# Sample rows of the ending ordered as (token, quarter) instead of (quarter, token)

## The chip, the cores and the metric

The kernel runs on one core of one Trainium2 chip. The metric is device time in microseconds, the median of repeated executions. Beside it there is one profiled execution of the kernel before, whose trace gives the time of every instruction and DMA packet.

## The reference

One step of a decoder layer on 256 prompt tokens and 32 sample tokens (8 sequences of 4 tokens), with 2048 features each. The two groups differ only in the state that they start from; the layer's last line is what the change touches:

```python
merged = jax.nn.sigmoid(m_a) * y_a + jax.nn.sigmoid(m_b) * y_b
x = layer_norm(ALPHA * x + merged @ w_o, ln1_g, ln1_b)
hid = jnp.square(jax.nn.relu(x @ w_up))
x = layer_norm(ALPHA * x + hid @ w_down, ln2_g, ln2_b)
...
def layer_norm(x, g, b):
    mu = jnp.mean(xf, -1, keepdims=True)
    var = jnp.mean(jnp.square(xf - mu), -1, keepdims=True)
    return ((xf - mu) * lax.rsqrt(var + LN_EPS) * g + b)
```

The results of this line are `y_prompt` (256 rows of 2048 floats, 2 MB) and `y_sample` (8 x 4 rows of 2048 floats, 256 KB). The convolution states and the delta-rule states are results too, and are stored much earlier.

## The kernel before

The kernel is one long stream of weight blocks. `add_group` lists them in order; each block is a 512 KB transfer on SP's queue (L171), a split of its floats into a high part on ScalarE (L179) and a low part on VectorE (L140), and three TensorE products for each 128 x 128 piece (L206 to L208). Activations lie with the features on the 128 partitions and the 288 tokens (256 of the prompt, then 32 samples) along the free axis. The order of the work is written out by hand: `at` and `due` say after which block a piece of other work is recorded, and each engine runs what it was given in that order.

The last layer norm needs the tokens on the partitions, so the features' tiles are turned by TensorE as they become ready. For the prompt this gives two tiles of 128 tokens x 2048 features. The 32 sample tokens would fill only 32 partitions; the kernel therefore packs them as 128 rows of 512 features, one row for each pair of a token and a quarter of the features. This packing is what the change reorders. Its steps, all in the ending:

- `tail_consts` (L561 on) loads, on GpSimd's queue, the scale and the shift of the layer norm. It is recorded 60 blocks before the last quarter of the `w_down` stream; GpSimd has nothing else to do by then and runs ahead of it. For the sample rows, `gs` and `bs` hold for each of the 128 rows the 512 values of its quarter.
- `sample_copy(w)` (L621, L622) copies 4 x 32 sample columns of `acc` to 128 columns of `cs` on ScalarE, four times; only `sample_copy(3)` has to wait for the last block.
- `sample_turn` turns these 128 x 128 pieces on TensorE (L627), takes their statistics (L631) and multiplies them by `gs`.
- `final` (from L648) combines the four rows of a token by a 128 x 128 matrix of quarters, `quart` (L722, L733), and ends with the sample rows' scaling (L740 on ScalarE, L741 on GpSimd, and VectorE's last instruction, recorded under its helper's line L143) and with their store, issued from ScalarE's queue (L750). The prompt's rows are stored from SP's queue: two stores of 512 KB (L708) and four of 256 KB (L713).

At the end of the program SP waits for the completion of each of these stores, one after the other (L1452).

Of the kernel before, what the change touches and what calls it, by code (L numbers as in the profile page):

```python
# [16 lines left out]
P = 128  # L17
D = 2048
NP_ = 256
NS = 32  # L20
NT = NP_ + NS
# [19 lines left out]
def _constants():  # L41
    k = np.arange(P)[:, None]
    m = np.arange(P)[None, :]
    f = {}
    f["ident"] = k == m
    f["lcum"] = (k <= m) & (k // 64 == m // 64)
    f["lrem"] = (k > m) & (k // 64 == m // 64)
    f["ones"] = np.ones((P, P))
    f["hm"] = k // 64 == m // 64
    i = np.arange(64)[None, :]  # L50
    f["lc"] = (k % 64) <= i
    f["mbias"] = np.where((k % 64) <= i, 0.0, -1e30)
    f["mask8"] = (k % 64) // 8 == i // 8
    f["i8"] = k % 8 == np.arange(8)[None, :]
    f["i8u"] = k % 8 < np.arange(8)[None, :]
    f["bo8"] = k // 8 == m // 8
    ks = k - 96
    mt = m % 32
    inb = (ks >= 0) & (ks // 4 == mt // 4)
    f["lcums"] = inb & (ks <= mt)  # L60
    f["lrems"] = inb & (ks > mt)
    f["lsp"] = ks == mt
    same = k // 4 == m // 4
    f["l4"] = same & (k <= m)
    f["mbias4"] = np.where(same & (k <= m), 0.0, -1e30)
    f["mask1s"] = same & (k % 2 == 0) & (m == k + 1)
    f["sel"] = (k // 32) == (np.arange(8)[None, :] % 4)
    f["bm3"] = (ks >= 0) & (ks // 4 == np.arange(8)[None, :])
    f["bmask"] = (k % 32) // 4 == np.arange(8)[None, :]
    f["hmask"] = (k // 64) == np.arange(2)[None, :]  # L70
    f["nlow"] = -np.concatenate([k // 64 == 1, (k // 32) % 2 == 1], 1).astype(np.float32)
    offs, cols, o = {}, [], 0
    f["quart"] = (k % 32 == m % 32) * 0.25
    f["rowhi"] = np.isin(k, (0, 2, 3, 5)) * 1.0
    f["rowlo"] = np.isin(k, (1, 4)) * 1.0
    early = ("hm", "bo8", "lcum", "lrem", "lcums", "lrems", "lsp", "bm3", "hmask")
    late = ("quart", "rowhi", "rowlo")
    for n, a in [(n, a) for n, a in f.items() if n not in early + late] + [(n, f[n]) for n in early + late]:
        if n in (early[0], late[0]):
            offs["early" if n == early[0] else "late"] = o  # L80
        a = np.broadcast_to(np.asarray(a, np.float32), (P, a.shape[1]))
        offs[n] = (o, o + a.shape[1])
        o += a.shape[1]
        cols.append(a)
    fm = np.ascontiguousarray(np.concatenate(cols, 1), dtype=np.float32)
    g = {}
    j = k % 64
    for s in (8, 16, 32):
        g[s] = (j // (2 * s) == i // (2 * s)) & ((j // s) % 2 == 0) & ((i // s) % 2 == 1)
    g["s"] = same & ((k // 2) % 2 == 0) & ((m // 2) % 2 == 1)  # L90
    io, cols, o = {}, [], 0
    for n, a in g.items():
        io[n] = (o, o + a.shape[1])
        o += a.shape[1]
        cols.append(np.asarray(a, np.int32))
    im = np.ascontiguousarray(np.concatenate(cols, 1), dtype=np.int32)
    return fm, offs, im, io


CF, CF_AT, CI, CI_AT = _constants()  # L100


@with_exitstack
def hybrid_kernel(ctx: ExitStack, tc: tile.TileContext, A):
# [31 lines left out]
    act, dve, pe, gps, sp = nc.scalar, nc.vector, nc.tensor, nc.gpsimd, nc.sync  # L136
# [5 lines left out]
    def stt(out, a, s, b, o0, o1):  # L142
        dve.scalar_tensor_tensor(out=out, in0=a, scalar=s, in1=b, op0=o0, op1=o1)  # L143
# [77 lines left out]
    ph = {}  # L221
# [325 lines left out]
    def collect(ps):  # L547
        turned(14)
        fin, bn = ph["fin"], ph["bn"]
        for b in range(2):  # L550
            dve.bn_aggr(out=fin[:, b, 1:3], in_=bn[:, b, 0:15])
        dve.tensor_scalar(out=fin[:, :, 2], in0=fin[:, :, 2], scalar1=15.0 * P, scalar2=None, op0=MUL)

        R = ph["R"] = ph["pool"].tile([P, 2, 2, 6], F32R, tag="mv", name="R")
        act.copy(R[:, 1, :, 3:5], bc(ones[:, 0:2], 2))
        act.mul(R[:, 1, :, 5], ones[:, 0:2], 0.0)
        sample_copy(2)
        idle = lambda: None
        fill.extend([idle] * 5 + [lambda: sample_turn(2, 3)])

    def tail_consts():  # L561
        g3 = ph["pool"].tile([P, KT, NT], F32, tag="R2", name="g3").rearrange("p k t -> p (k t)")
        ph["g2"] = g3[:, 0:D]
        ph["gs"], ph["bs"], ph["b0"] = (g3[:, D + 512 * u:D + 512 * u + 512] for u in range(3))
        ph["late"] = g3[:, D + 1536:D + 1536 + CF.shape[1] - NL]
        gps.dma_start(ph["g2"][:, 1024:D], A["ln2_g"][:, 1024:D].to_broadcast([P, D - 1024]))
        gps.dma_start(ph["b0"], A["ln2_b"][:, 1024:1536].to_broadcast([P, 512]))
        gps.dma_start(ph["late"], A["cf"][:, NL:])
        for j in range(4):
            for t, n in (("gs", "ln2_g"), ("bs", "ln2_b")):  # L570
                gps.dma_start(ph[t][32 * j:32 * j + 32, :], A[n][:, 512 * j:512 * j + 512].to_broadcast([32, 512]))

    def tail_tiles():
        pl = ph["pool"]
# [44 lines left out]


    def sample_copy(w):  # L621
        act.copy(ph["cs"][:, w * P:w * P + P].rearrange("p (j t) -> p j t", j=4), ph["acc"][:, w::4, NP_:NT])  # L622

    def sample_turn(w0, w1, split=False):
        g = gtile()[:, 0:(w1 - w0) * P]
# [15 lines left out]
    def out_tiles(p):  # L641
        for u in range(2):
            turned(2 * p + u)
        if p == 6:
            sample_copy(0)
            sample_copy(1)

    def final(ps):  # L648
        a, fin, sm, Y, Ys, R = ph["acc"], ph["fin"], ph["sm"], ph["Y"], ph["Ys"], ph["R"]
# [26 lines left out]
        m = mv[:, :, 0]  # L676
# [70 lines left out]
        dve_unit(0, 3, r03)  # L747
        dve_unit(1, 3, r13)
        stt(Ys, ph["gs"], ts, Ys, MUL, ADD)
        act.dma_start(A["y_sample"].rearrange("b t (j f) -> j (b t) f", j=4), Ys)  # L750

    mark["up"] = len(blocks)
    for c in range(4):
# [586 lines left out]
    t = raw.pop(0)  # L1340
# [31 lines left out]
    for i in range(3, len(blocks)):  # L1372
# [47 lines left out]
        if i == mark["down3"] - 60:  # L1420
            tail_consts()
# [34 lines left out]
```

## Time and profile before

| | |
|---|---|
| median of 3 executions | 1706.29 us (1705.9 to 1706.83) |
| the profiled execution: time | 1707.11 us |
| the profiled execution: span of the trace | 1705.3 us |
| TensorE busy | 1688.1 us, 99% of the span |
| VectorE, ScalarE, GpSimd busy | 59%, 43%, 8% |

The span is the time from the first to the last instruction in the trace; what the execution's time has beyond it, 1.8 us, lies outside the trace. Times inside the trace count from the span's start. A queue's row gives its packets, the megabytes that they carried, and the share of the 16 DMA engines' time that they took; q1 carries SP's transfers, q10 those of ScalarE, q0 those of GpSimd.

### The profile page before, as it was taken

Reading aid. Unit: us, or ns where it says so; the run is one execution under the profiler, and the core shown is the slowest. Engines: PE = TensorE matmul, PEld = TensorE weight load, DVE = VectorE, ACT = ScalarE, POOL = GpSimd, SP = SyncE. Lnnn points to the kernel's source line nnn. Section 1 sums busy time; section 2 is a strip of 40 time slices with the busy share of each in tenths; the row PEclk is TensorE's granted clock in tenths of the full one; section 3 lists DMA queues with packets and bytes.
Section 4 is the critical chain, followed back from the end, with each engine's and each line's share of the span. In section 5 each row is a group of like instructions: output and inputs, shape, how many; then the busy total and the mean of one; then the engine's idle time right before and its main releaser. Section 6 shows DMA issues by size and latency. Waiting matters only on the chain.

```text
span 1705.3 us, 31096 instructions
## 1 busy us (share of the span) xinstructions
PE 1688.1 (99%) x13063; PEld 1669.0 (98%) x13063; DVE 1008.3 (59%) x1297; ACT 734.5 (43%) x1068; POOL 131.3 (8%) x220
## 2 busy tenths in 40 slices
PE   9999999999999999999999999999999999999996
PEld 7999999999999999999999999999999999999996
DVE  4577885757544445556788744565445654466564
ACT  4775536334543333344445533344334433344432
POOL 2232421023300000000010000000000000000000
PEclk8999999999999999999999999999999999999998
DMA  8464366435655555555565555555555555555551
GB/s 243 139 196 138 123 190 201 148 112 168 182 164 171 161 167 167 162 161 163 171 185 171 169 163 167 167 161 167 168 161 164 169 161 169 165 161 165 166 158 63
DMA packets 274654, 279.18 MB, mean 164 GB/s; under 512 B 13072, under 2 KB 269521, under 8 KB 274509
## 3 DMA queue, kind: packets, MB, share of 16 engines
q1 hardware_dynamic: 270126, 265.82, 50.3%
q0 software_dynamic: 4256, 11.12, 2.4%
q8 instruction: 102, 1.67, 0.4%
q10 hardware_dynamic: 132, 0.26, 0.1%
q14 instruction: 38, 0.30, 0.0%
HBM read 269.68 MB, written 7.48 MB: 163 GB/s over the span
## 4 chain that ended last, share of the span: by engine, by line
PE 98%; DMA 0%; DVE 0%; SPq 0%; issue 0%; ACT 0%
PE acc L206 31%; PE acc L208 31%; PE acc L207 31%; PE g L1085 1%; DMA xr<-in_x_prompt_dram 0%; PE g L1073 0%; PE g L1232 0%; PE g L1252 0%; PE g L1255 0%; PE g L832 0%; PE g L799 0%; PE g L606 0%; PE g L1204 0%; PE g L1244 0%; PE g L959 0%; PE g L800 0%
## 5 line engine op out<-in xcount | busy, mean ns | idle before, releaser
L140 DVE TENSOR_TENSOR lo<-raw,hi 128x1024 fp32r<-128x1024 f32 (+2 forms) x502 | 614.7, 1227 | 551.7 <-ACT hi L179 549.1
L179 ACT CAST hi<-raw 128x1024 fp32r<-128x1024 f32 (+1 forms) x498 | 517.5, 1041 | 761.7 <-PE acc L207 709.2
L206 PE MATMUL acc<-xh,hi 128*128 128x288 f32 x1408 | 422.6, 300 | 0.0
L208 PE MATMUL acc<-xh,lo 128*128 128x288 f32 x1408 | 416.8, 296 | 0.0
L207 PE MATMUL acc<-xl,hi 128*128 128x288 f32 x1408 | 416.5, 296 | 0.0
L206 PE MATMUL acc<-dh,hi 128*128 128x290 f32 x1024 | 303.9, 297 | 0.0
L207 PE MATMUL acc<-dl,hi 128*128 128x290 f32 x1024 | 303.3, 296 | 0.0
L208 PE MATMUL acc<-dh,lo 128*128 128x290 f32 x1024 | 302.7, 296 | 0.0
L208 PE MATMUL acc<-hh,lo 128*128 128x288 f32 x1024 | 302.3, 295 | 0.0
L206 PE MATMUL acc<-hh,hi 128*128 128x288 f32 x1024 | 302.3, 295 | 0.0
L207 PE MATMUL acc<-hl,hi 128*128 128x288 f32 x1024 | 302.2, 295 | 0.0
L206 PEld LDWEIGHTS acc<-xh,hi 128*128 128x128 f32 x1408 | 265.5, 189 | 2.4 <-issue 0.7
L207 PEld LDWEIGHTS acc<-xl,hi 128*128 128x128 f32 x1408 | 265.9, 189 | 0.9
L208 PEld LDWEIGHTS acc<-xh,lo 128*128 128x128 f32 x1408 | 265.6, 189 | 0.0
L206 PEld LDWEIGHTS acc<-dh,hi 128*128 128x128 f32 x1024 | 193.6, 189 | 0.1
L208 PEld LDWEIGHTS acc<-dh,lo 128*128 128x128 f32 x1024 | 193.3, 189 | 0.0
L207 PEld LDWEIGHTS acc<-dl,hi 128*128 128x128 f32 x1024 | 193.3, 189 | 0.1
L207 PEld LDWEIGHTS acc<-hl,hi 128*128 128x128 f32 x1024 | 192.4, 188 | 0.0
L208 PEld LDWEIGHTS acc<-hh,lo 128*128 128x128 f32 x1024 | 192.3, 188 | 0.0
L206 PEld LDWEIGHTS acc<-hh,hi 128*128 128x128 f32 x1024 | 192.1, 188 | 0.0
L207 PE MATMUL acc<-ml,hi 128*128 128x288 f32 x256 | 75.6, 295 | 0.0
L208 PE MATMUL acc<-mh,lo 128*128 128x288 f32 x256 | 75.6, 295 | 0.0
(402 smaller groups left out, 1619.8 us busy)
## 6 DMA issues: line engine op xcount, KB each, us to landing
raw<-in_w_in_dram SPq DMA_DIRECT2D x176, 512.0 KB, 3.5
raw<-in_w_up_dram SPq DMA_DIRECT2D x128, 512.0 KB, 3.8
raw<-in_w_down_dram SPq DMA_DIRECT2D x128, 512.0 KB, 3.6
raw<-in_w_o_dram SPq DMA_DIRECT2D x32, 512.0 KB, 3.6
raw<-in_w_a_out_dram SPq DMA_DIRECT2D x16, 512.0 KB, 3.7
raw<-in_w_b_out_dram SPq DMA_DIRECT2D x16, 512.0 KB, 3.6
S<-in_state_gdn_dram POOLq DMA_DIRECT2D x8, 512.0 KB, 7.5
out_dram<-S POOLq DMA_DIRECT2D x8, 512.0 KB, 4.4
```

The source lines that it names most:

```text
L140: dve.tensor_tensor(out=out, in0=a, in1=b, op=op)
L179: act.copy(his[i][:, k:k + step], raw[i][:, k:k + step])
L206: pe.matmul(o, wh, xh_, start=st, stop=False)
L207: pe.matmul(o, wh, xl_, start=False, stop=False)
L208: pe.matmul(o, wl, xh_, start=False, stop=en)
L1085: pe.matmul(out[r, q * 64:q * 64 + 64], a[r, q, :], b[r, q, :], start=True, stop=True)
```

## The change

The 128 sample rows are numbered as 4 x token + quarter instead of 32 x quarter + token. Four things follow from it: the matrix `quart` sums over neighbours instead of over rows 32 apart; the scale and the shift are loaded by one transfer each, whose source repeats the four quarters 32 times, instead of four transfers each; ScalarE's copy writes its 128 columns with a step of four floats instead of one after another; and the output is addressed as 128 rows of 512 floats that follow one another in memory, instead of as 4 x 32 rows with 8 KB between rows of one quarter.

```diff
-    f["quart"] = (k % 32 == m % 32) * 0.25
+    f["quart"] = (k // 4 == m // 4) * 0.25
...
-        for j in range(4):
-            for t, n in (("gs", "ln2_g"), ("bs", "ln2_b")):
-                gps.dma_start(ph[t][32 * j:32 * j + 32, :], A[n][:, 512 * j:512 * j + 512].to_broadcast([32, 512]))
+        for t, n in (("gs", "ln2_g"), ("bs", "ln2_b")):
+            gps.dma_start(ph[t], A[n].rearrange("o (j f) -> o j f", j=4).to_broadcast([NS, 4, 512]))
...
-        act.copy(ph["cs"][:, w * P:w * P + P].rearrange("p (j t) -> p j t", j=4), ph["acc"][:, w::4, NP_:NT])
+        act.copy(ph["cs"][:, w * P:w * P + P].rearrange("p (t j) -> p j t", j=4), ph["acc"][:, w::4, NP_:NT])
...
-        act.dma_start(A["y_sample"].rearrange("b t (j f) -> j (b t) f", j=4), Ys)
+        act.dma_start(A["y_sample"].rearrange("b t (j f) -> (b t j) f", j=4), Ys)
```

As built, the store's destination is [128 rows, 512 floats] where it was [4, 32, 512]; every engine has its instructions in the same order as before, but for GpSimd, which issues six loads fewer. The changed kernel has one source line less from L569 on, so that the store stands at L749.

## The prediction

> **What bounds the kernel now.** I read the page's chain first, then the end of the chain in order of time, then the stages of the ending, and last the DMA packets and the issues of the stores.
>
> ```profile
> span 1705.3 us, 31096 instructions
> q10 hardware_dynamic: 132, 0.26, 0.1%
> PE 98%; DMA 0%; DVE 0%; SPq 0%; issue 0%; ACT 0%
> ...
> 1692.88 0.74 DVE Y L143
> 1693.62 0.68 DVE r L143
> ```
>
> TensorE carries 98% of the chain and the change takes nothing from it. But the chain in order of time ends with VectorE at 1693.62 + 0.68 = 1694.30, 11 us before the span does. No engine computes in those 11 us. The stages of the ending show what they hold:
>
> ```profile
> core 0: us, PE busy (x) PEld busy (x) DVE busy (x) ACT busy (x) POOL busy (x), PEclk, DMA share, GB/s
> 1693.40:1697.60 4.20, 0.00 (x0) 0.00 (x0) 0.89 (x2) 0.00 (x0) 0.11 (x1) 0.50 0.96 362
> 1697.70:1698.90 1.20, 0.00 (x0) 0.00 (x0) 0.00 (x0) 0.00 (x0) 0.00 (x0) 0.50 0.37 41
> 1698.90:1700.90 2.00, 0.00 (x0) 0.00 (x0) 0.00 (x0) 0.00 (x0) 0.00 (x0) 0.50 0.69 167
> 1700.90:1702.60 1.70, 0.00 (x0) 0.00 (x0) 0.00 (x0) 0.00 (x0) 0.00 (x0) 0.50 0.22 83
> 1702.60:1703.84 1.24, 0.00 (x0) 0.00 (x0) 0.00 (x0) 0.00 (x0) 0.00 (x0) 0.50 0.09 36
> 1703.84:1705.30 1.46, 0.00 (x0) 0.00 (x0) 0.00 (x0) 0.00 (x0) 0.00 (x0) 0.50 0.00 0
> ```
>
> The last two columns are the busy share of the 16 DMA engines and the rate. Until 1697.6 they are full (0.96, 362 GB/s). Then comes a hole of 1.2 us at 41 GB/s, then two microseconds at 167, and from 1700.9 to 1703.84 a thin tail: 0.22 of 16 engines is 3.5 engines, 0.09 is 1.4. After the last packet 1.46 us of waits and drains follow. So the end is set by a few DMA engines that work on after the others are done. Which, the packets say. First the window of one prompt store alone (128 rows of 2 KB, issued from SP at 1690.54), then the thin tail:
>
> ```profile
> DMA packets 144, 0.26 MB, mean 97 GB/s; under 512 B 16, under 2 KB 16, under 8 KB 144
> q1 hardware_dynamic: 144, 0.26, 26.1%
> ...
> DMA packets 102, 0.19 MB, mean 42 GB/s; under 512 B 11, under 2 KB 11, under 8 KB 102
> q1 hardware_dynamic: 66, 0.12, 7.0%
> q10 hardware_dynamic: 36, 0.07, 4.0%
> ```
>
> The prompt store is 144 packets: 128 rows and 16 small ones. The sample store, of the same 128 rows and 0.26 MB, is 132 (the q10 row of the page): 128 rows and 4 small ones. I read a small packet as one engine's completion: the prompt store runs on 16 engines with 8 rows each, the sample store on 4 with 32 rows each. In the thin tail 11 small packets are left. Four engines that owe three stores each (the sample rows and the last two prompt stores) would owe 12; that fits, and so do the 3.5 engines above. The four do sample rows while the prompt rows in their queues wait, and the last prompt store ends at 1703.84 because of them.
>
> The Trainium skill ("DMA: Bandwidth & Descriptors", section "Why a DMA increments its semaphore by 16 and not by 1") gives the rule behind this: a transfer issued from SP or ScalarE uses the largest number of engines up to 16 that divides the slowest dimension of both sides, and each engine used posts one completion. By that rule [4, 32, 512] against 128 partitions takes 4 engines and [128, 512] takes 16; the 4 and 16 small packets above agree for the two shapes that this trace has.
>
> **The change part by part.**
>
> *The output's transfer.* It keeps its 128 rows, its place (ScalarE issues it behind VectorE's last instruction at 1694.3) and its queue. Its built form is that of the prompt store, 128 rows of 512 floats on both sides, so I take 16 engines with 8 rows each. Removed from each of the four engines: 32 - 8 = 24 rows. Added to each of the twelve: 8. One row costs 0.261 x 16 x 2.7 us = 11.3 us of engine time over 128 rows = 0.088 us (the prompt store's window, 2.7 us long). So the four lose 2.1 us and the twelve gain 0.70 us. What is late next is the twelve engines' own end, 1700.9 by the windows. How far that moves depends on the hole, and so on when the last prompt store's packets arrive:
>
> ```profile
> 1690.54 0.37 SPq L713 DMA_DIRECT2D out_dram<-Y  x1
> 1693.77 0.65 SPq L713 DMA_DIRECT2D out_dram<-Y  x1
> 1694.33 1.15 ACTq L750 DMA_DIRECT2D out_dram<-r  x1
> 1694.52 1.14 SPq L713 DMA_DIRECT2D out_dram<-Y  x1
> 1695.75 1.58 SPq L713 DMA_DIRECT2D out_dram<-Y  x1
> ```
>
> The same instruction takes 0.37 us on an idle queue, 0.65 us behind two 512 KB stores, and 1.14 and 1.58 us once the sample store is in the queue. No row shows it behind a 16-engine sample store. The bounds are 0.65 us (the delay came from four engines that could not take 32 rows each) and 1.58 us (it comes from two queues issuing at once). I take 0.65, as it is the nearest row: a store of this form behind a full backlog of 16-engine stores. Then the last issue ends at 1695.75 + 0.65 = 1696.40 instead of 1697.33, 0.93 us earlier, and its packets could begin at 1698.9 - 0.93 = 1697.97. Before them each engine now has 8 sample rows: the full stretch ends at 1697.6 + 0.70 = 1698.30, so the last store begins there, 0.60 earlier than now, with no hole. Its eight rows per engine take 0.70 us at the pace of the lone store, or the 2.0 us that the twelve took (1698.9 to 1700.9). Ends: 1699.0 or 1700.3; bytes give a check: 41 x 1.2 + 167 x 2.0 + 83 x 1.7 + 36 x 1.24 = 569 KB are left at 1697.7, and at 362 GB/s that is 1.57 us, end 1699.3. I take the middle, 1699.7. Gain: 1703.84 - 1699.7 = 4.1 us, between 3.5 and 4.8. The 1.46 us behind the last packet stay, since the same stores are waited for.
>
> *The loads of scale and shift.*
>
> ```profile
> L571 POOL DMA_DIRECT2D g<-in_ln_g_dram x4: 496/497/518, 864.1 to 870.9; - x4
> L571 POOL DMA_DIRECT2D g<-in_ln_b_dram x4: 496/498/515, 864.6 to 871.4; - x4
> POOL r L588 <- PE acc L207: 707.7, 1, 707.7
> ```
>
> Eight issues of 0.5 us become two, so 3 us of GpSimd's time go, for the same 512 KB. GpSimd then waits 707.7 us for TensorE (the third row, who waited for whom): nothing is queued behind them, and the values are needed 800 us later. Worth 0; without that cover it would be the 3 us. The stream of weights passes there with the same bytes: 0.
>
> *ScalarE's copy with a step of four floats.*
>
> ```profile
> L179 ACT CAST hi<-raw 128x1024 fp32r<-128x1024 f32 x492 | 514.1, 1046 | 757.5 <-PE acc L207 709.2 <-issue 39.2 <-ACT hi L179 8.7
> L179 ACT CAST hi<-raw 128x512 fp32r<-128x512 f32 x6 | 3.4, 619 | 4.2 <-DMA raw<-in_w_in_dram 4.2
> L622 ACT COPY r<-acc x4: 293/298/300, 1674.3 to 1685.8; 128x128 f32<-128x128 f32 x4
> ...
> PEld g L686 <- DVE R L140: 0.4, 1, 0.4
> ```
>
> An element costs (1046 - 619) / 512 = 0.83 ns, so 128 of them 0.107 us of the copy's 0.298. No row here has this step. Bounds: no change, or each element twice, +0.11 us for each of four copies; it cannot gain, as the count stays. Only the last copy, at 1685.8, has TensorE behind it, and there TensorE waits 0.4 us for VectorE's R soon after (the last row), which takes up 0.11. I take 0; without that cover +0.1.
> The Trainium skill speaks against this part ("SBUF — State Buffer", section "Door 1: The DMA port swizzle"): full rate needs at least two consecutive accesses to one 16-byte line, and each step to a new line pays. A step of four floats is a new line every time; the page has no price for it, so by it the sum would lose the 0.1 us that the doubled copy stands for, if the cover failed. No run here shows the penalty.
>
> *The matrix of quarters, the turns, statistics and scalings* keep their shapes and their order: 0.
>
> Sum: -4.1 us. The profiled execution would go from 1707.11 to 1703.0, with a span of 1701.2. Its time stands 0.82 above the median 1706.29, so the median comes to 1702.2.
>
> **The rivals.**
>
> *The issues stay slow.* The hole is due to two queues issuing at once, whatever the shape; for it speaks that the 1.14 us issue overlaps ScalarE's own of 1.15 us almost wholly, against it that the 1.58 us one comes when ScalarE's is over. Then the last store's packets come at 1698.9 as now, and the twelve engines' end stays: 1700.9 if the 8 added rows fit in the hole (0.70 in 1.2 us), 1701.6 if they follow. Gain 2.9 to 2.2 us, median 1703.4 to 1704.1.
>
> *The path to memory is slow, not the engines.* After the hole the rate is 167 GB/s even while more than four engines work (share 0.69). If that is the limit, spreading the rows does not raise it: 569 - 49 = 520 KB after 1698.9 take 3.1 us, end 1702.0, gain 1.8 us, median 1704.5. Against it: 362 GB/s before the hole, of the same kind of stores.
>
> *Slower: the store falls on one engine.* Its destination is now one run of 256 KB. If it went out as such, from one engine, 128 x 0.088 = 11.3 us and two prompt stores' 16 rows (1.4 us) from 1697.0 on end at 1709.7: 5.9 us later, median 1712.2. It decides only at one engine; on two, 64 + 16 rows end at 1704.0, no change. Against it: the built form has 128 rows on both sides, as the 144-packet store has.
>
> *The change doesn't do what it says* (still four engines): gain 0; against it, the same built form.
>
> **How the numbers follow.** Some 0.2%, 3.4 us, is what a measurement of this kernel can tell from no change. Chances: forecast 0.58 (3.5 to 4.8 us, all over the bound), issues stay slow 0.26, slow path 0.09, no change 0.03, one engine 0.04. So faster 0.58, same 0.38, slower 0.04. The forecast's own range is 1701.5 to 1702.8; the range goes to 1701.0 for the executions' spread (0.4 to 0.5 us to either side) and at the other end over the slow issues to 1704.4, which leaves out the last three.
>
> **What would show it.** Right: q10 with 144 packets, 16 of them small; no tail below four engines' share; the last L713 issue near 0.65 us and no hole after 1697.6; last packet near 1699.7; ScalarE's copy at 0.30 us. Wrong: 132 packets, or fewer; the last issue still at 1.6 us with the hole in place, which would be the second case; a hole gone but a rate near 167 GB/s, the third.

## The result

The changed kernel takes 1702.06 us (median of 11 executions, 1700.99 to 1702.92), the kernel before 1705.9 us beside it (11 executions): a ratio of 0.9977, 95% interval 0.9968 to 0.9986, so 3.8 us less. The profiled execution took 1702.91 us, with a span of 1701.1 us. The page's first line, and its row for ScalarE's queue:

```profile
span 1701.1 us, 31087 instructions
...
q10 hardware_dynamic: 144, 0.26, 0.0%
```

The sample store is now 128 rows and 16 small packets, where it had 4. The stages of the ending, cut at the times used before (last two columns: share of the 16 DMA engines, GB/s):

```profile
core 0: us, PE busy (x) PEld busy (x) DVE busy (x) ACT busy (x) POOL busy (x), PEclk, DMA share, GB/s
1693.40:1697.60 4.20, 0.00 (x0) 0.00 (x0) 1.21 (x2) 0.22 (x1) 0.42 (x1) 0.50 0.89 345
1697.70:1698.90 1.20, 0.00 (x0) 0.00 (x0) 0.00 (x0) 0.00 (x0) 0.00 (x0) 0.50 1.03 382
1698.90:1700.90 2.00, 0.00 (x0) 0.00 (x0) 0.00 (x0) 0.00 (x0) 0.00 (x0) 0.50 0.20 76
1700.90:1702.60 1.70, 0.00 (x0) 0.00 (x0) 0.00 (x0) 0.00 (x0) 0.00 (x0) 0.50 0.00 0
```

The second row was the hole: it went from 41 to 382 GB/s. The tail after 1700.9 is empty. Cut where this kernel's own work begins and ends:

```profile
1692.60:1693.70 1.10, 0.31 (x1) 0.00 (x0) 1.10 (x2) 1.02 (x2) 1.10 (x1) 0.50 0.00 0
...
1697.60:1699.44 1.84, 0.00 (x0) 0.00 (x0) 0.00 (x0) 0.00 (x0) 0.00 (x0) 0.50 0.95 352
1699.44:1701.10 1.66, 0.00 (x0) 0.00 (x0) 0.00 (x0) 0.00 (x0) 0.00 (x0) 0.50 0.00 0
```

The engines are full to the last packet at 1699.44, which was at 1703.84. The waits and drains behind it take 1.66 us, 0.2 more than before. Of the issues of the stores, only ScalarE's fell back to the idle queue's 0.37 us; the last one from SP, at 1696.06, takes 1.12 us:

```profile
1694.08 0.66 SPq L712 DMA_DIRECT2D out_dram<-Y  x1
1694.64 0.37 ACTq L749 DMA_DIRECT2D out_dram<-r  x1
1694.84 1.14 SPq L712 DMA_DIRECT2D out_dram<-Y  x1
1696.06 1.12 SPq L712 DMA_DIRECT2D out_dram<-Y  x1
```

One part of the change costs something. First the copy's row, TensorE's turn behind it and GpSimd's loads; then the chain's last line:

```profile
L621 ACT COPY r<-acc x4: 414/422/428, 1674.5 to 1686.1; 128x128 f32<-128x128 f32 x4
...
1686.52 0.33 PE L626 MATMUL g<-cf,r 128*128 128x128 f32 x1 [0.21 <-ACT r L621]
...
1689.68 0.15 DVE L140 TENSOR_TENSOR r<-r,g 128x1 f32<-128x1 f32 x1
...
L570 POOL DMA_DIRECT2D g<-in_ln_g_dram x1: 566/566/566, 864.3 to 864.3; - x1
L570 POOL DMA_DIRECT2D g<-in_ln_b_dram x1: 588/588/588, 864.9 to 864.9; - x1
...
1693.92 0.68 DVE r L143
```

Each copy takes 0.42 us where it took 0.30, and TensorE waits 0.21 us for the last one. VectorE ends at 1694.60, 0.30 us later than before. Of this, 0.20 is there already at VectorE's first instruction behind the last block and comes from the long stream, as other traces differ too. The other 0.10 enters at VectorE's small instruction of 1689.68 (before: 1689.38): it reads the product of `quart`, which TensorE runs in order behind the late turn.

### The profile page after: what moved, and what is told of

Its sections match the earlier page's. It is cut to its first block, busy times and chain, and to the rows that moved or that the text cites. A ratio compares the mean times of both kernels' runs of the same rounds, so it can differ in the third digit from the quotient of the medians.

```text
span 1701.1 us, 31087 instructions
## 1 busy us (share of the span) xinstructions
PE 1688.0 (99%) x13063; PEld 1669.1 (98%) x13063; DVE 1008.2 (59%) x1297; ACT 734.5 (43%) x1068; POOL 128.3 (8%) x214
## 4 chain that ended last, share of the span: by engine, by line
PE 98%; DMA 0%; DVE 0%; SPq 0%; issue 0%; ACT 0%
PE acc L206 31%; PE acc L208 31%; PE acc L207 31%; PE g L1084 1%; DMA xr<-in_x_prompt_dram 0%; PE g L1072 0%; PE g L1231 0%; PE g L1251 0%; PE g L1254 0%; PE g L831 0%; PE g L798 0%; PE g L605 0%; PE g L1203 0%; PE g L1243 0%; PE g L958 0%; PE g L799 0%
```

## The experiments

The long stream, which no edit here touches, ends up to 2.8 us apart from trace to trace (the first 512 KB prompt store is issued between 1690.90 and 1693.68), so the endings are compared by the time from the issue of the first 512 KB prompt store to the last packet. It is 11.1 us in the kernel before (1692.76 to 1703.84) and 6.4 us in the changed one (1693.07 to 1699.44).

**The old rows on 16 engines.** The kernel before with one edit:

```diff
-        act.dma_start(A["y_sample"].rearrange("b t (j f) -> j (b t) f", j=4), Ys)
+        ys = A["y_sample"].rearrange("b t (j f) -> j (b t) f", j=4)
+        for j in range(4):
+            act.dma_start(ys[j], Ys[32 * j:32 * j + 32, :])
```

> The kernel before, with its old row order, its eight loads and its copy, but the sample store cut into four stores of 32 rows each (one quarter each, still 8 KB between rows), so that each has 32 rows on both sides and, by my theory, runs on 16 engines with 2 rows each. Theory (the number of engines is the whole gain): no tail after the hole, last packet near 1699.4, median 1702.0, some 3.8 us under the kernel before; q10 shows 128 rows and 64 small packets. Rival (the gain comes from rows that follow one another in memory): the rows are 8 KB apart as before, so the tail stays and the median is that of the kernel before, 1705.9, or above it for three more issues of 0.37 us.

Measured: 1702.5 us against 1706.3 us, ratio 0.9976 (0.9967 to 0.9986), the changed kernel's gain. Its q10 row and its stages:

```profile
q10 hardware_dynamic: 192, 0.26, 0.1%
...
1693.40:1697.60 4.20, 0.00 (x0) 0.00 (x0) 0.80 (x2) 0.00 (x0) 0.01 (x1) 0.50 0.99 354
1697.60:1699.64 2.04, 0.00 (x0) 0.00 (x0) 0.00 (x0) 0.00 (x0) 0.00 (x0) 0.50 0.89 300
1699.64:1701.20 1.56, 0.00 (x0) 0.00 (x0) 0.00 (x0) 0.00 (x0) 0.00 (x0) 0.50 0.00 0
```

192 packets are 128 rows and 4 x 16 small ones. The ending is 7.0 us, with rows still 8 KB apart and no hole. So 4.1 of the 4.7 us by which the changed kernel's ending is shorter come without rows that follow one another in memory, and without the row order, the loads and the copy of the change. The ending stays 0.6 us longer than the changed kernel's, at 300 GB/s to the end where that has 352; whether this is the rows' distance or the four issues from ScalarE, no run parts.

**The new rows on 4 engines.** The changed kernel with

```diff
-        act.dma_start(A["y_sample"].rearrange("b t (j f) -> (b t j) f", j=4), Ys)
+        ys = A["y_sample"].rearrange("b t (j f) -> (b t j) f", j=4)
+        for r in (slice(0, 124), slice(124, P)):
+            act.dma_start(ys[r], Ys[r, :])
```

> The changed kernel with its new row order, loads and copy, but the store cut into rows 0 to 123 and rows 124 to 127. Neither 124 nor 4 is divided by a number from 5 to 16, so each should run on 4 engines: 31 rows and 1 row on each, in memory one after another. Theory (number of engines): the tail of four engines is back, last packet near 1703.9, median 1706.0 (that of the kernel before, and 0.1 us for the slower copy); q10 has 128 rows and 8 small packets. Rival (rows that follow one another): as the changed kernel, 1702.1.

Measured: 1705.83 against 1706.3 us, ratio 0.9998 (0.9988 to 1.0008): the gain is gone. This trace's stream ends 1.9 us early, so its stages are cut 1.9 us earlier:

```profile
q10 hardware_dynamic: 136, 0.26, 0.1%
...
1691.50:1695.70 4.20, 0.00 (x0) 0.00 (x0) 0.93 (x2) 0.00 (x0) 0.15 (x1) 0.50 0.95 357
1695.85:1697.05 1.20, 0.00 (x0) 0.00 (x0) 0.00 (x0) 0.00 (x0) 0.00 (x0) 0.50 0.52 102
1697.05:1699.05 2.00, 0.00 (x0) 0.00 (x0) 0.00 (x0) 0.00 (x0) 0.00 (x0) 0.50 0.55 152
1699.05:1701.41 2.36, 0.00 (x0) 0.00 (x0) 0.00 (x0) 0.00 (x0) 0.00 (x0) 0.50 0.16 60
```

136 packets are 128 rows and 2 x 4 small ones. Full, then a slump, then the thin tail (0.16 of 16 engines is 2.6): the shape of the kernel before, and an ending of 10.5 us. These two runs are the two halves of the answer: with 16 engines the old rows have nearly the whole gain, with 4 the new rows have next to none (0.6 us of the ending, nothing that the times can tell).

**The new rows on one engine.** The same edit with 127 in place of 124.

> The changed kernel with the store cut into rows 0 to 126 and row 127: 127 is a prime, so one engine should take 127 rows, and again one the last row. Theory (the end is the busiest engine's rows at 0.088 us each): 128 x 0.088 = 11.3 us and two prompt stores' 16 rows, 1.4 us, from 1697.0 on: last packet near 1709.7, median 1711.8, 5.9 us above the kernel before; q10 has 128 rows and 2 small packets. Rival (the tail of the kernel before was the hole and the slow issues, not the rows per engine): no later than the kernel before, 1705.9.

Measured: 1713.39 against 1706.3 us, ratio 1.0039 (1.0024 to 1.0054): 7.1 us slower by the medians, 6.7 by the ratio, for an estimate of 5.9. The tail:

```profile
q10 hardware_dynamic: 130, 0.26, 0.0%
...
1698.90:1702.60 3.70, 0.00 (x0) 0.00 (x0) 0.00 (x0) 0.00 (x0) 0.00 (x0) 0.50 0.07 25
1702.60:1709.10 6.50, 0.00 (x0) 0.00 (x0) 0.00 (x0) 0.00 (x0) 0.00 (x0) 0.50 0.07 26
```

Two small packets, and for ten microseconds 0.07 of 16 engines, which is one, at 26 GB/s: 0.079 us for a row of 2 KB. Just before, from 1697.3 to 1698.9, this engine moves only six rows, 8 GB/s. That the number of engines follows from the rows, 16 for 32 or 128 of them, 4 for 124 or for 4, one for 127, is what the Trainium skill states ("DMA: Bandwidth & Descriptors", section "Why a DMA increments its semaphore by 16 and not by 1"); the 64 and 8 small packets of these runs agree, and of the 2 here one is the 127 rows'. The other shows that the single row went out on one engine too.

**The old store behind the prompt's, on SP's queue.** The kernel before with `act.dma_start` of the sample rows turned into `sp.dma_start`.

> The kernel before with its four-engine sample store issued from SP's queue behind the six prompt stores instead of from ScalarE's. It parts the hole from the tail. Theory (the hole comes from the four engines' rows standing ahead of the last prompt store): with the sample store last there is no hole, all prompt rows are out near 1698.3, and then four engines do 32 rows each, 2.8 us: last packet 8.3 to 8.6 us after the issue of the first 512 KB store (before 11.1, changed 6.4), median 1703.7, about 2.6 us under the kernel before. Rival (the tail alone, 32 rows on four engines, makes the whole difference): the last packet stays 10.5 us or more after that issue and the median within 0.1% of the kernel before.

Measured: 1705.28 against 1706.51 us, ratio 0.9994 (0.9985 to 1.0004), an ending of 10.1 us (1691.33 to 1701.38). The theory on the hole falls. The rival has the time, which can't be told from the kernel before's, but not the ending, which it put at 10.5 us or more.

```profile
1691.95:1697.00 5.05, 0.00 (x0) 0.00 (x0) 0.91 (x2) 0.00 (x0) 0.12 (x1) 0.50 0.96 366
1697.00:1698.90 1.90, 0.00 (x0) 0.00 (x0) 0.00 (x0) 0.00 (x0) 0.00 (x0) 0.50 0.25 28
1698.90:1701.38 2.48, 0.00 (x0) 0.00 (x0) 0.00 (x0) 0.00 (x0) 0.00 (x0) 0.50 0.22 79
1701.38:1702.90 1.52, 0.00 (x0) 0.00 (x0) 0.00 (x0) 0.00 (x0) 0.00 (x0) 0.50 0.00 0
```

All prompt rows are out at 1697.0, at 366 GB/s. Then the four engines are alone, with nothing ahead of them and one queue only, and still their first 1.9 us move 28 GB/s at a busy share of 0.25 (4 engines); after that they move 79. The sample rows take 4.4 us where 32 x 0.088 = 2.8 were reckoned. So the hole belongs to the store on four engines itself: it starts slowly. In those 1.9 us the four are busy all the time and move 26 rows (28 GB/s), so a row takes 0.25 x 16 x 1.9 / 26 = 0.29 us. The store on one engine began as slowly. Why a store on few engines does so is open. The ending is 3.7 us longer than the changed kernel's for two reasons: 24 rows more on each of the four engines, 2.1 us, and the slow start, 4.4 - 2.8 = 1.6 us.

**The copy turned round.** The changed kernel, where the copy reads with a step and writes without one:

```diff
-        act.copy(ph["cs"][:, w * P:w * P + P].rearrange("p (t j) -> p j t", j=4), ph["acc"][:, w::4, NP_:NT])
+        act.copy(ph["cs"][:, w * P:w * P + P].rearrange("p (t j) -> p t j", j=4),
+                 ph["acc"][:, w::4, NP_:NT].rearrange("p j t -> p t j"))
```

(The written side names the 128 columns as token and quarter, both in memory order. The step on the read side is 4 x 288 = 1152 floats, as it takes every fourth of `acc`'s tiles of 288 columns; the expectation below says 288.)

> The changed kernel with ScalarE's copy turned round: it writes its 128 columns one after another and steps through acc by 288 floats when it reads; the values are the same. Theory (a step of four floats on the written side costs the 0.12 us that each copy became longer): the copies are back at 0.30 us, TensorE no longer waits for the last one, and the scaled sample rows are 0.1 us earlier against the end of the stream. Rival (a step costs on either side): the copies stay at 0.42 us or get longer.

Measured, by the profile alone: no gain, the rival holds.

```profile
L621 ACT COPY r<-acc x4: 409/419/432, 1675.2 to 1686.7; 128x128 f32<-128x128 f32 x4
...
PE g L627 <- ACT r L621: 0.2, 1, 0.2
```

The second row is from the table of who waited for whom. On the read side the step costs the same 0.12 us.

**Without the sample store.**

```diff
-        act.dma_start(A["y_sample"].rearrange("b t (j f) -> (b t j) f", j=4), Ys)
...
+        gps.dma_start(A["y_sample"].rearrange("b t (j f) -> (b t j) f", j=4), ph["gs"])
```

> The changed kernel without its sample store at the end: the output y_sample gets the 128 rows of gs instead, stored by GpSimd more than 100 us earlier, so the sample result is left out; all else is the same. Theory (the ending of the changed kernel is held by the bytes that go out after 1693.7, evenly over 16 engines): 256 KB less at 362 GB/s is 0.7 us, median 1701.4 if the changed kernel has 1702.1; and the last two prompt stores are still issued in 1.1 us each, since these issues wait for a backlog and not for ScalarE's queue. Rival (two queues issuing at once make the issues slow): without ScalarE's store they fall to the 0.65 us of the store before them, and the last packet comes 1 us earlier or more.

Measured: 1701.05 us, ratio 0.9971 (0.996 to 0.9982); the changed kernel, run on the same chip, had 1701.9 us and 0.9973 (0.9965 to 0.9982), so the medians are 0.85 apart and the intervals can't part them. The traces can: the ending is 5.7 us for 6.4.

```profile
1693.79 0.71 SPq L713 DMA_DIRECT2D out_dram<-Y  x1
1694.60 1.14 SPq L713 DMA_DIRECT2D out_dram<-Y  x1
1695.84 0.62 SPq L713 DMA_DIRECT2D out_dram<-Y  x1
...
1693.70:1698.50 4.80, 0.00 (x0) 0.00 (x0) 0.92 (x2) 0.00 (x0) 0.00 (x0) 0.50 0.99 382
1698.50:1700.20 1.70, 0.00 (x0) 0.00 (x0) 0.00 (x0) 0.00 (x0) 0.00 (x0) 0.50 0.00 0
```

The bytes' 0.7 us is met. On the issues both theories were half right: the last one falls to 0.62 us without ScalarE's store, the one before stays at 1.14. The end doesn't follow them, only the bytes.

**The sample store on SP's queue**, in the changed kernel (`sp.dma_start` for `act.dma_start`).

> The changed kernel with the sample store issued from SP's queue, behind the six prompt stores, instead of from ScalarE's. Theory (held by bytes): the order of the bytes changes and not their number; the last packet stays within 0.3 us of the changed kernel's, 6.4 us after the issue of the first 512 KB store, and the stores from the fourth on are issued in 1.1 us each although no second queue is at work. Rival (two queues slow each other): those issues fall to 0.65 us.

```profile
1692.27 0.70 SPq L712 DMA_DIRECT2D out_dram<-Y  x1
1693.07 1.15 SPq L712 DMA_DIRECT2D out_dram<-Y  x1
1694.31 0.62 SPq L712 DMA_DIRECT2D out_dram<-Y  x1
1695.03 0.58 SPq L749 DMA_DIRECT2D out_dram<-r  x1
```

Measured, by the profile alone: an ending of 6.35 us (1691.31 to 1697.66), as the theory of bytes had it. One queue issues faster, but for one 1.15, and nothing is gained.

**The prompt's halves early.** The changed kernel with

```diff
-            if n:
-                sp.dma_start(A["y_prompt"][0, b * P:(b + 1) * P, 0:1024], Y[:, b, 0:1024])
+            sp.dma_start(A["y_prompt"][0, b * P:(b + 1) * P, c], Y[:, b, c])
```

> The changed kernel with each 512 KB prompt store cut into its two halves, the first issued as soon as ScalarE has written it, some 2 us before the second is ready; eight prompt stores of 256 KB instead of four and two of 512 KB. In the changed kernel's trace the DMA engines are idle from 1692.6 to 1693.7 and half busy in the 1.4 us before. Theory (the ending is held by bytes): 512 KB move into that idle time, the full stretch after 1693.7 shrinks by up to 450 KB, 1.2 us: 0.07% under the changed kernel, median 1700.9 where that has 1702.1. Rival (SP's issues set the end: eight of them, 1.1 us each when they pile up): the last issue comes no earlier, gain under 0.3 us.

Measured: 1700.95 us, ratio 0.9968 (0.9956 to 0.9981), and in a second measurement 1700.78 against 1706.51 us, 0.9967 (0.9954 to 0.9979); the changed kernel beside the first had 1701.9.

```profile
1693.72 0.39 SPq L711 DMA_DIRECT2D out_dram<-Y  x1
1694.20 0.40 SPq L711 DMA_DIRECT2D out_dram<-Y  x1
1694.69 0.43 SPq L711 DMA_DIRECT2D out_dram<-Y  x1
...
1692.60:1693.70 1.10, 0.00 (x0) 0.00 (x0) 1.10 (x3) 0.67 (x2) 0.86 (x1) 0.67 0.85 311
1693.70:1697.84 4.14, 0.00 (x0) 0.00 (x0) 0.55 (x1) 0.00 (x0) 0.00 (x0) 0.50 1.00 369
1697.84:1699.40 1.56, 0.00 (x0) 0.00 (x0) 0.00 (x0) 0.00 (x0) 0.00 (x0) 0.50 0.00 0
```

The idle stretch of the changed kernel (1692.6 to 1693.7 at 0 GB/s) now moves 311, and the ending shrinks to 5.1 us (1692.71 to 1697.84). No issue is slow any more. The trace and both medians show about 1 us more gain than the change alone brings; the intervals of the ratios overlap, so the times alone don't show it.

## Why the prediction held, step by step

*Four engines set the end.* Right, and shown from both sides: 16 engines with the old rows take 0.9976 of the time before, 4 engines with the new rows 0.9998. What the step did not have is that the rows of a store on few engines are slow themselves at first, 0.29 us each where it reckoned 0.088.

*The twelve others' end, without a hole.* The hole did go, but not for the reason given. The step took the last issue from 1.58 to 0.65 us and drew the packets 0.93 us earlier from that. That issue measured 1.12 us, and the runs without ScalarE's issue show that the end doesn't hang on it. The 1.14 us of the issue before it, which the prediction put down to the sample store, stand even where there is none. The hole was the slow start of the four-engine store itself.

*The last store's pace.* The middle between 0.70 and 2.0 us was too slow. The engines run full to the end: 352 GB/s after 1697.6. The 2.0 us were no pace of the prompt store as such: by that window's share and rate a row took 0.69 x 16 x 2.0 us / 163 rows = 0.135 us beside the four-engine store, and in the changed kernel, from 1697.6 on, 0.95 x 16 x 1.84 us / 316 rows = 0.088. The check by bytes (1699.3) was a better term than the middle, 1699.7; counted from VectorE's end the last packet comes 4.84 us later, for 9.54 before, a gain of 4.7 where 4.1 was reckoned.

*The copy.* Taken as 0, it cost 0.10. The price was a little over its upper bound (0.12 us a copy, for 0.11), and the cover failed. The wait for `R` stands only before the second pair of R's turns. The first pair, which waited for nothing, starts 0.33 us later (1687.67 before, 1688.00 after), as TensorE's order puts it behind the late turn; ScalarE's cast of it follows 0.32 later, and behind that cast come a product (1688.53, now 1688.83) and then the product of `quart` (1688.95, now 1689.26), on which VectorE waits. Of these delays 0.20 is the stream's own. The Trainium skill spoke against this step ("SBUF — State Buffer", section "Door 1: The DMA port swizzle"), and the trace agrees that stepping over 16-byte lines costs: 0.12 us for 128 elements, about 1 ns each.

*The loads.* 0, as reckoned: two issues of 0.57 and 0.59 us for eight of 0.50, on an engine that waits long after them.

*Sum.* The span fell by 4.2 us: 4.7 in the DMA tail, less 0.3 by which VectorE ended later (0.2 of it the stream's own), less 0.2 in the waits behind the last packet. The reckoned 4.1 is near it because what it left out, VectorE's later end and the longer waits, 0.5 together, made up for most of the tail's extra 0.6. So the mechanism was right, but that the sum came out so near is luck.

*The rivals.* Slow issues and a slow path to memory both needed a hole or a low rate after 1697.6; neither is there, though the last issue did stay slow. The store on one engine, built as an experiment, is somewhat worse than priced: 7.1 us for 5.9.

## What to carry to other kernels

Count a transfer's small packets before reckoning its time: in these runs they told on how many engines it ran, and a last store whose slowest dimension was 4 kept four engines at work when the others were done. Reordering it to 128 rows and cutting it into stores of 32 rows both put it on 16 engines; that the rows follow one another in memory was not needed for most of the gain. Once all engines were full to the last packet, faster issues brought nothing; fewer bytes at the end did, and so, by the trace, did bytes moved into earlier idle time, as the early halves show.

## What the runs showed of the hardware beyond that

A store with 32 rows on each of four engines starts slowly even when it is alone: 28 GB/s for 1.9 us, then 79. One with 127 rows on one engine does too: 8 GB/s for 1.6 us, then 25 to 26. The second of the 256 KB prompt stores behind the two of 512 KB is issued in 1.14 to 1.15 us in every ordering tried, but in 0.40 us once the 512 KB stores are halved; the cause was not looked for, since no end hung on it. And ScalarE's copy pays the same for a step whether it reads or writes with it.
